# Pooled differences in PSUM, accumulating weight transfers from negated raw weights, and one scaling operation for two conv halves, in a one-core decoder layer

## The chip, the cores and the metric

The kernel runs on one core of one Trainium2 chip. The metric is the device time of one execution in microseconds, the median of the runs. A core has TensorE (PE, with PEld for its weight loads), VectorE (DVE), ScalarE (ACT), GpSimd (POOL) and SyncE (SP); each engine works through its own queue in order.

## The reference

One inference step of a one-layer trunk on 288 tokens: 256 of a new sequence, and 8 requests with 4 tokens each that carry a history. All in fp32.

```python
h = rmsnorm(x, norm1_g)
proj = h @ w_in + b_in                       # 2048 -> 1024 a, 1024 gate, 1024 z
u = a * sigmoid(gate)
c = silu(layernorm(depthwise_causal_conv([hist_conv, u], conv_w, conv_b), ln_g, ln_b))   # 31 taps
# z in 4 groups of 256 channels, windows 2, 4, 8, 16:
d = (sum of the last w of [hist_pool, z]) / min(w, position + 1) - z
p = (d @ pool_w[group]) * pool_scale
x = x + [c, p] @ w_out                       # 2048 -> 2048
f = relu(rmsnorm(x, norm2_g) @ w_ff1) ** 2   # 2048 -> 8192
x = x + f @ w_ff2
y = rmsnorm(x, norm_f)
```

The outputs are y and the last rows of [hist_conv, u] and [hist_pool, z].

## The kernel before, in words

Channels lie on the 128 partitions and the 288 tokens (T) along the free axis. Each fp32 product is made of three products of a narrower type, F32R: every weight tile and every activation is split into a high half `hi` (a cast) and a low half `lo` (the value less `hi`), and `gemm` (matmuls on line 292) adds hi x hi, lo x hi and hi x lo in PSUM. A matmul takes a 128x128 weight tile and 128x288 activations.

Weights come as raw halves of 128x1024, loaded by SyncE's queue (`load`), and are split by `split_part`. The cast to `hi` is always ScalarE's (line 260). The letter in the table WAYS says who makes `lo`: G is two GpSimd subtractions of 128x512 (line 269), V one VectorE subtraction (line 265), and D negates `hi` on ScalarE (line 262) and then lets a transfer issued by GpSimd read the raw half again from memory and add it (line 263). A product of the first layer takes four halves, so "GDGV" for c6 gives a way to each of its four. There are twelve D halves: one in c3 and c4, two in p3, c5, p2 and p1, one in c6 and p0. The raw and the split tiles come from pools of 6 and 5 buffers, so a weight is split as soon as TensorE has done with the one five before.

The first layer's products follow a written list:

```python
SEQUENCE = [(_s[0], int(_s[1])) for _s in "c0 c1 c2 c3 c4 p3 c5 p2 P3 c6 p1 P2 p0 P1 c7 P0".split()]
```

c_i is the product of conv pair i (128 channels of a in one bank, 128 of gate in the other), p_g that of pool group g, P_g the product of group g's pooled differences with `pool_w`. A c or p product has 96 matmuls, a P product 12. P1 runs inside c7, between its blocks (`between`), and P0 inside the first product of the output projection. All matmuls up to there are held in program order (`chain`); some products take their first matmuls in an order written by hand (TURN: c2, c5, the first of the projection, and others).

After c_i, `conv_pair` scales both banks by the row 1/rms (`rb`, line 434, two VectorE operations of 128x288), makes the sigmoid and u, and `taps` adds the 31 taps of the convolution, 30 VectorE operations of 128x256 (line 459), and those of the 32 sample tokens through a GpSimd product `prd` (line 463) and a VectorE reduction (line 465). The taps have a late priority and fill VectorE's gaps.

After p_g, `pool_group` scales (line 482), adds the bias into `z_all` (lines 485, 486), and GpSimd doubles the windows: sums `s` of 2, 4, 8, 16 (line 491). Then come a correction of the first positions, the scaling of the new samples' sums (line 497) and their difference into `d` (line 498). VectorE writes the other 256 tokens of `d` (line 500), ScalarE casts `d` to `dh` (line 502), VectorE subtracts to `dl` (line 503). `d` is an SBUF tile of the tag "ag2". `pool_products` multiplies and evacuates the two banks `pp` (lines 514 and 515, one ScalarE and one VectorE operation for each).

PSUM holds two tiles of two banks for products (`acc`), the tap sums and c1's banks (`cvp`), and a single tile of two banks with the tag "ms" for the pool products and the norms' sums.

A framework schedules the program: it keeps the data dependencies and lays out each engine's instructions by priority and by times that it models. The order on an engine is fixed when the kernel is built. `issue_after` pins one instruction behind another. After this stage (some 215 us) come the rest of the output projection and the feed-forward part in four chunks; the diff doesn't touch them.

Of the kernel before, what the change touches and what calls it, by code (L numbers as in the profile page):

```python
# [9 lines left out]
F32 = mybir.dt.float32  # L10
F32R = mybir.dt.float32r
AF = mybir.ActivationFunctionType
# [4 lines left out]
P = 128  # L17
D = 2048
# [51 lines left out]
TURN = "110100" * 4 + "01" * 6 + "1100" * 3  # L70


WAYS = {"c2": "GVGV", "c3": "GDGG", "c4": "GGGD", "c5": "GDGD", "c6": "GDGV", "c": "GGGV", "p0": "GDVG", "p": "GDDG", "w0": "GV", "w": "GG", "ff": "VV"}


VEC = (("norm1_g", 16), ("b_in", 24), ("conv_b", 8), ("ln_g", 8), ("ln_b", 8), ("pool_scale", 8), ("norm2_g", 16), ("norm_f", 16))
# [10 lines left out]
def trunk_kernel(ctx: ExitStack, tc: tile.TileContext, io):  # L87
# [18 lines left out]
    def nm(s):  # L106
        seen[s] = seen.get(s, 0) + 1
        return f"{s}{seen[s]}"
# [22 lines left out]
    def ms(name):  # L131
        return msp.tile([P, 2, 512], F32, name=nm(name), tag="ms")

    def f32(t):
        return t.bitcast(F32)

    def both(r):

        return r[:, None, :T].to_broadcast([P, 2, T])
# [114 lines left out]
    def split_part(raw, src, hi, lo, way):  # L254

        nc.scalar.copy(hi, raw)  # L260
        if way == "D":
            nc.scalar.activation(lo, f32(hi), AF.Copy, scale=-1.0)
            added.append(nc.gpsimd.dma_start(lo, src, accum_op=ALU.add))
        elif way == "V":
            nc.vector.tensor_tensor(lo, raw, f32(hi), op=ALU.subtract)  # L265
        else:
            for j in range(0, raw.shape[1], 2):
                with tc.issue_after(pooled[-1].ins) if pooled else nullcontext():
                    nc.gpsimd.tensor_tensor(lo[:, j : j + 2, :], raw[:, j : j + 2, :], f32(hi[:, j : j + 2, :]), op=ALU.subtract)  # L269
# [27 lines left out]
    def gemm(banks, rhs, m_outer=False, between={}, classes="", by_part=False, gets=None, pairs=None, late=0):  # L297


        n = len(rhs)  # L300
        gets = gets or ready.pop(0)
        todo, begins = [], {}
        if by_part:
            for k in range(0, n, 2):
                sets = [range(len(banks))] if k else [range(2), range(2, len(banks))]
                for last, ms_ in enumerate(sets, 1 - len(sets)):
                    for part, (w, x) in enumerate(((0, 0), (1, 0), (0, 1))):
                        if last == 0:
                            begins[len(todo)] = (k, None, k + 1)[part]
                        todo += [(k + (1 - d if x else d), m, w, x) for m in ms_ for d in range(2)]  # L310
        else:
            pairs = pairs or [(k, m) for k in range(0, n, 2) for m in range(len(banks))]
            if m_outer:
                pairs.sort(key=lambda km: km[1])
            for k, m in pairs:
                begins[len(todo)] = (k, m) if m else k
                todo += [(k + d, m, w, x) for d, w, x in ((0, 0, 0), (1, 0, 0), (0, 1, 0), (1, 1, 0), (1, 0, 1), (0, 0, 1))]
        todo[:late] = sorted(todo[:late], key=lambda p: p[2])
        head = todo[: len(classes)]
        for j, c in enumerate(classes):  # L320
            todo[j] = next(p for p in head if c == "." or (p[0] + p[3]) % 2 == int(c))
            head.remove(todo[j])
        ends = {m: [f(j for j, p in enumerate(todo) if p[1] == m) for f in (min, max)] for m in range(len(banks))}
        ahead = None
        for j, (k, m, w, x) in enumerate(todo):
            if begins.get(j) in between:
                ahead = between[begins[j]]()
            with tc.issue_after(ahead.ins) if ahead is not None and not chain else nullcontext():
                last = mm(banks[m][:, :T], gets[k // 8](k % 8, m)[w], rhs[k][x], start=j == ends[m][0], stop=j == ends[m][1])
        ready.extend(itertools.islice(weights, 1))  # L330
        return last.ins

    def bank2():
        return acc.tile([P, 2, 512], F32, name=nm("ac"), tag="ac")

    def each(bk):
        return [bk[:, m, :] for m in range(2)]
# [84 lines left out]

    def conv_products(i, **kw):
        history(i)
        banks = each(bank2())
        gemm(banks, hx, **kw)
        return banks

    def conv_pair(i, banks):
        up = u_all[:, i, 0:UO]  # L430
        us = samples(u_all[:, i, UO:UL], US)
        ta, gate = [b[:, :T] for b in banks]
        for b in (gate, ta):
            nc.vector.tensor_tensor(b, b, rb, op=ALU.mult)
        tg = tmpp.tile([P, 2, T], F32, name=nm("tg"), tag="ag", bufs=2)[:, 0, :]
        nc.scalar.activation(tg, gate, AF.Sigmoid, bias=v("b_in", 8 + i))
        for out, a, b in ((up[:, CH:UO], ta[:, :SEQ], tg[:, :SEQ]), (us[:, :, CH:US], samples(ta[:, SEQ:T], NS), samples(tg[:, SEQ:T], NS))):
            nc.vector.scalar_tensor_tensor(out=out, in0=a, scalar=v("b_in", i), in1=b, op0=ALU.add, op1=ALU.mult)
        if i % 2 == 0:
            cs.append(actp.tile([P, 2, T], F32, name=nm("c"), tag="c", bufs=4))  # L440
        while waiting:
            taps(*waiting.pop())
        if i in (2, 3):
            waiting.append((i, up, us))
        else:
            taps(i, up, us)
# [24 lines left out]
                    nc.gpsimd.tensor_tensor(sum_c[:, 0, :], sum_c[:, 0, :], part, op=ALU.add)  # L471


    dd = {}

    def pool_group(g):
        nc.sync.dma_start(z_all[:, 2 * g : 2 * g + 2, ZO:ZL], io["hist_p"][:, 2 * g : 2 * g + 2, :])
        bk = bank2()
        gemm(each(bk), hx)
        z = z_all[:, 2 * g : 2 * g + 2, :]  # L480
        tz = tmpp.tile([P, 2, T], F32, name=nm("tz"), tag="ag", bufs=2)
        nc.vector.tensor_tensor(tz, bk[:, :, :T], both(rb), op=ALU.mult)
        for m in range(2):
            b_in = v("b_in", 16 + 2 * g + m)
            nc.scalar.activation(z[:, m, PH:ZO], tz[:, m, 0:SEQ], AF.Identity, bias=b_in)
            nc.scalar.activation(samples(z[:, m, ZO:ZL], ZS)[:, :, PH:ZS], samples(tz[:, m, SEQ:T], NS), AF.Identity, bias=b_in)
        s, w = z, 1
        while w < WINDOWS[g]:
            s2 = tmpp.tile([P, 2, ZL], F32, name=nm("s"), tag="s", bufs=2)
            for m in range(2):  # L490
                nc.gpsimd.tensor_tensor(s2[:, m, 2 * w - 1 :], s[:, m, 2 * w - 1 :], s[:, m, w - 1 : ZL - w], op=ALU.add)  # L491
            s, w = s2, 2 * w
        d = tmpp.tile([P, 2, T], F32, name=nm("d"), tag="ag2", bufs=2)
        first_sums = s[:, :, PH : PH + w - 1]
        nc.gpsimd.tensor_tensor(first_sums, first_sums, rcnt[:, None, w - 2 : 2 * w - 3].to_broadcast([P, 2, w - 1]), op=ALU.mult)
        news = [x[:, :, ZO:ZL].rearrange("p m (b t) -> p m b t", t=ZS)[:, :, :, PH:] for x in (s, z)]
        nc.gpsimd.tensor_scalar(news[0], news[0], 1.0 / w, None, op0=ALU.mult)
        last = nc.gpsimd.tensor_tensor(d[:, :, SEQ:T].rearrange("p m (b t) -> p m b t", t=NS), news[0], news[1], op=ALU.subtract)
        newest[g] = last
        nc.vector.scalar_tensor_tensor(out=d[:, :, 0:SEQ], in0=s[:, :, PH:ZO], scalar=1.0 / w, in1=z[:, :, PH:ZO], op0=ALU.mult, op1=ALU.subtract)  # L500
        dh, dl = act2("dx", tag="p", bufs=4)
        nc.scalar.copy(dh, d)
        nc.vector.tensor_tensor(dl, d, f32(dh), op=ALU.subtract)  # L503
        dd[g] = dh, dl
# [12 lines left out]

    for i in range(2):
        history(i)
    pair0 = each(bank2())  # L520
    pair1 = [cvp.tile([P, 512], F32, name=nm("ac"), tag="cv") for m in range(2)]

    def first_row():
# [2 lines left out]
    chain.append(gemm(pair0 + pair1, hx, between={15: first_row}, classes="01" * 18 + TURN, by_part=True))  # L526
    third = conv_products(2, classes=TURN)
    nc.gpsimd.memset(z_all[:, :, 0:PH], 0.0)
    conv_pair(0, pair0)
    conv_pair(1, pair1)  # L530
    conv_pair(2, third)
    def ahead(n):

        while len(ready) < n + 1:
            ready.extend(itertools.islice(weights, 1))
        return ready.pop(n)

    for kind, i in SEQUENCE[3:-1]:
        if (kind, i) == ("P", 1):
            continue  # L540
        if i == 7:
            pooled.append(newest[1])
        if kind == "c":
            conv_pair(i, conv_products(i, classes=TURN if i == 5 else "", **(dict(gets=ahead(1), between={8: lambda: pool_products(1)}) if i == 7 else {})))
        elif kind == "p":
            pool_group(i)
        else:
            pooled.append(newest[i])
            pool_products(i)
    pooled.append(newest[0])  # L550
    proj = [halves(dd[k // 2])[k % 2] for k in korder]
    bks = [bank2() for _ in range(2)]
# [248 lines left out]
```

## Time and profile before

| | before |
|---|---|
| median of 3 runs | 1084.95 us (1084.92 to 1085.11) |
| profiled execution | 1083.8 us, its span 1082.0 us |
| granted TensorE clock | 0.998 |
| busy: PE, DVE, ACT, POOL | 1068.6, 632.2, 484.2, 179.8 us |
| GpSimd's transfers (queue q0) | 1728 packets, 6.29 MB |

The span is from the first to the last instruction of the profiled execution. Its own time is 1.15 us under the median of the runs, so sums made on the profile are set against 1083.8 and then carried to the median as differences. Times in rows are microseconds from the start of the span. A window's row gives its length, TensorE's busy time with the count of matmuls, the granted clock, the share of time that the transfer engines were busy, and GB/s.

### The profile page before, as it was taken

What the parts mean: (1) busy time and instruction counts of PE and PEld (TensorE: products, weight loads), DVE (VectorE), ACT (ScalarE), POOL (GpSimd) and SP (SyncE); (2) the same over time, 40 slices, a digit from 0 to 9 for tenths busy, and PEclk for the clock granted to TensorE, in tenths of its full rate; (3) what the DMA queues carried; (4) which work ended last, traced back from release to release, by engine and by line L of the source; (5) the groups of instructions that cost most, each with busy time, mean ns of one, the idle gap of its engine ahead of it and who ended that gap; (6) DMA issues with size and microseconds to landing.
All of it is one profiled execution on the core that took longest, in us unless ns stands there. A gap on an engine that the chain in (4) does not pass through costs nothing.

```text
span 1082.0 us, 19548 instructions
## 1 busy us (share of the span) xinstructions
PE 1068.6 (99%) x8176; PEld 1067.0 (99%) x8176; DVE 632.2 (58%) x804; ACT 484.2 (45%) x593; POOL 179.8 (17%) x189
## 2 busy tenths in 40 slices
PE   9999999999999999999999999999999999999996
PEld 8999999999999999999999999999999999999996
DVE  8899998788655544444544444545544445554552
ACT  8655555565544433334443333444433334444441
POOL 1898889612000000000000000000000000000001
PEclk9999999999999999999999999999999999999999
DMA  9898778555555555555555555555555555555522
GB/s 328 279 267 222 198 173 249 189 168 170 170 169 165 174 171 163 174 168 165 175 171 163 173 168 166 173 172 164 172 171 163 173 172 163 172 169 166 172 79 88
DMA packets 59017, 193.34 MB, mean 179 GB/s; under 512 B 6320, under 2 KB 11312, under 8 KB 58928
## 3 DMA queue, kind: packets, MB, share of 16 engines
q1 hardware_dynamic: 56336, 184.35, 54.4%
q0 software_dynamic: 1728, 6.29, 3.2%
q8 instruction: 64, 1.05, 0.4%
q10 hardware_dynamic: 864, 1.44, 0.4%
q14 instruction: 25, 0.20, 0.1%
HBM read 187.78 MB, written 4.28 MB: 177 GB/s over the span
## 4 chain that ended last, share of the span: by engine, by line
PE 75%; issue 20%; DVE 2%; DMA 1%; POOL 1%; ACT 0%; SPq 0%; POOLq 0%; DVEq 0%
PE ac L292 74%; DMA wlo<-in_w 1%; DMA wr<-in_w 1%; DVE pc L459 1%; PE pp L292 0%; POOL wlo L269 0%; DVE wlo L265 0%; POOL s L491 0%; POOL xT L737 0%; DVE dx L503 0%; DVE z_all L409 0%; SPq L191 0%; ACT z_all L407 0%; DVE wlo L360 0%; DVE c L465 0%
## 5 line engine op out<-in xcount | busy, mean ns | idle before, releaser
L260 ACT CAST whi<-wr 128x1024 fp32r<-128x1024 f32 (+1 forms) x332 | 346.7, 1044 | 549.9 <-PE ac L292 538.3
L265 DVE TENSOR_TENSOR wlo<-wr,whi 128x1024 fp32r<-128x1024 f32 x282 | 348.3, 1235 | 348.0 <-ACT whi L260 348.0
L292 PE MATMUL ac<-ax,whi 128*128 128x288 f32 x2048 | 351.0, 292 | 0.0
L292 PE MATMUL ac<-fx,whi 128*128 128x288 f32 x2048 | 350.2, 292 | 0.0
L292 PEld LDWEIGHTS ac<-ax,whi 128*128 128x128 f32 x2048 | 296.1, 187 | 0.0
L292 PEld LDWEIGHTS ac<-fx,whi 128*128 128x128 f32 x2048 | 295.5, 187 | 0.0
L292 PE MATMUL ac<-ax,wlo 128*128 128x288 f32 x1024 | 217.4, 292 | 0.0
L292 PE MATMUL ac<-fx,wlo 128*128 128x288 f32 x1024 | 216.4, 292 | 0.0
L292 PEld LDWEIGHTS ac<-ax,wlo 128*128 128x128 f32 x1024 | 162.6, 187 | 0.0
L292 PEld LDWEIGHTS ac<-fx,wlo 128*128 128x128 f32 x1024 | 162.2, 187 | 0.0
L737 POOL TENSOR_TENSOR xT<-xT,rf 128x288 f32<-128x288 f32 x4 | 3.1, 793 | 799.9 <-ACT rf L741 799.9
L292 PE MATMUL ac<-hx,whi 128*128 128x288 f32 x768 | 131.1, 294 | 1.3 <-DVE hx L354 1.3
L292 PEld LDWEIGHTS ac<-hx,whi 128*128 128x128 f32 x768 | 111.6, 188 | 1.7 <-ACT hx L356 1.5
L269 POOL TENSOR_TENSOR wlo<-wr,whi 128x512 fp32r<-128x512 f32 x76 | 103.7, 1449 | 21.8 <-ACT whi L260 20.3
L459 DVE SCALAR_TENSOR_TENSOR pc<-u_all,vec,pc 128x256 f32<-128x256 f32 x232 | 100.1, 482 | 3.5 <-ACT pc L456 1.9
L292 PE MATMUL ac<-hx,wlo 128*128 128x288 f32 x384 | 80.4, 295 | 2.0 <-DMA wlo<-in_w 1.7
L292 PEld LDWEIGHTS ac<-hx,wlo 128*128 128x128 f32 x384 | 60.7, 188 | 2.7 <-DMA wlo<-in_w 2.2
L292 PE MATMUL ac<-dx,whi 128*128 128x288 f32 x256 | 46.2, 295 | 0.0
L292 PE MATMUL ac<-mx,whi 128*128 128x288 f32 x256 | 44.5, 292 | 0.0
L679 DVE SCALAR_TENSOR_TENSOR t<-ac,r 128x576 f32<-128x576 f32 x32 | 24.2, 758 | 25.4 <-PE ac L292 25.3
L292 PEld LDWEIGHTS ac<-dx,whi 128*128 128x128 f32 x256 | 38.2, 188 | 0.2
L292 PEld LDWEIGHTS ac<-mx,whi 128*128 128x128 f32 x256 | 37.4, 187 | 0.0
(129 smaller groups left out, 541.7 us busy)
## 6 DMA issues: line engine op xcount, KB each, us to landing
wr<-in_w SPq DMA_DIRECT2D x335, 512.0 KB, 3.8
wlo<-in_w POOLq DMA_DIRECT2D x12, 512.0 KB, 7.7
xT<-in_xT SPq DMA_DIRECT2D x8, 288.0 KB, 7.2
wr<-in_w SPq DMA_DIRECT2D x5, 256.0 KB, 4.8
out_u_out<-u_all SPq DMA_DIRECT2D x1, 1208.0 KB, 10.1
u_all<-in_hist_c SPq DMA_DIRECT2D x8, 136.0 KB, 5.8
out_z_out<-z_all SPq DMA_DIRECT2D x1, 668.0 KB, 8.7
z_all<-in_hist_p SPq DMA_DIRECT2D x4, 152.0 KB, 8.4
```

What stands on the lines that cost most here:

```text
L260: nc.scalar.copy(hi, raw)
L265: nc.vector.tensor_tensor(lo, raw, f32(hi), op=ALU.subtract)
L269: nc.gpsimd.tensor_tensor(lo[:, j : j + 2, :], raw[:, j : j + 2, :], f32(hi[:, j : j + 2, :]), op=ALU.subtract)
L292: last = nc.tensor.matmul(*args, **kw)
L459: nc.vector.scalar_tensor_tensor(out=dst, in0=up[:, w : w + SEQ], scalar=cwv[:, w : w + 1], in1=pc, op0=ALU.mult, op1=ALU.add)
L679: nc.vector.scalar_tensor_tensor(out=t, in0=bk[:, :, :T], scalar=0.0, in1=both(rows2[0]), op0=ALU.max, op1=ALU.mult)
L737: eng.tensor_tensor(xk, xk, r[:, None, :].to_broadcast([P, n, T]), op=ALU.mult)
```

## The change

- `split_part`, way D: `lo` is the negated raw half, written ahead of the cast to `hi`; before, it was the negated `hi`, written behind it. The transfer that adds the raw half onto `lo` stays.
- WAYS: the entry of c6 is gone, so that c6 takes "GGGV" of "c": its second half goes from D to G.
- `conv_products` and `conv_pair`: where both banks lie in one tile, one VectorE operation of 128x576 scales them. c1, whose banks are two tiles, stays as it was.
- `pool_group` ends with GpSimd's difference of the new samples, written into `s` itself. The rest goes to a new function `pool_means`: `d` is a PSUM tile of the tag "ms", ScalarE copies the new samples into it, VectorE writes the other tokens, and `dh` and `dl` are made from there.
- The means of group 3 follow p3; those of groups 2 and 1 follow the products P3 and P2; those of group 0 follow P1. P1 runs ahead of block 4 of c7; before, it ran ahead of block 8.

```diff
-WAYS = {..., "c5": "GDGD", "c6": "GDGV", "c": "GGGV", ...}
+WAYS = {..., "c5": "GDGD", "c": "GGGV", ...}
...
+        if way == "D":
+            nc.scalar.activation(lo, raw, AF.Copy, scale=-1.0)
         nc.scalar.copy(hi, raw)
         if way == "D":
-            nc.scalar.activation(lo, f32(hi), AF.Copy, scale=-1.0)
             added.append(nc.gpsimd.dma_start(lo, src, accum_op=ALU.add))
...
-        ta, gate = [b[:, :T] for b in banks]
-        for b in (gate, ta):
-            nc.vector.tensor_tensor(b, b, rb, op=ALU.mult)
+        if isinstance(banks, list):
+            ta, gate = [b[:, :T] for b in banks]
+            for b in (gate, ta):
+                nc.vector.tensor_tensor(b, b, rb, op=ALU.mult)
+        else:
+            nc.vector.tensor_tensor(banks[:, :, :T], banks[:, :, :T], both(rb), op=ALU.mult)
+            ta, gate = [banks[:, m, :T] for m in range(2)]
...
-        last = nc.gpsimd.tensor_tensor(d[:, :, SEQ:T]..., news[0], news[1], op=ALU.subtract)
-        newest[g] = last
-        nc.vector.scalar_tensor_tensor(out=d[:, :, 0:SEQ], in0=s[:, :, PH:ZO], scalar=1.0 / w, in1=z[:, :, PH:ZO], op0=ALU.mult, op1=ALU.subtract)
+        newest[g] = nc.gpsimd.tensor_tensor(news[0], news[0], news[1], op=ALU.subtract)
+        sums[g] = s, z, news[0], 1.0 / w
+
+    def pool_means(g):
+
+        s, z, fresh, scale = sums[g]
+        d = ms("d")[:, :, :T]
+        nc.scalar.copy(d[:, :, SEQ:T].rearrange("p m (b t) -> p m b t", t=NS), fresh)
+        nc.vector.scalar_tensor_tensor(out=d[:, :, 0:SEQ], in0=s[:, :, PH:ZO], scalar=scale, in1=z[:, :, PH:ZO], op0=ALU.mult, op1=ALU.subtract)
         dh, dl = act2("dx", tag="p", bufs=4)
         nc.scalar.copy(dh, d)
         nc.vector.tensor_tensor(dl, d, f32(dh), op=ALU.subtract)
...
+    def last_pool():
+
+        pool_products(1)
+        pool_means(0)
...
-            conv_pair(i, conv_products(i, ..., **(dict(gets=ahead(1), between={8: lambda: pool_products(1)}) if i == 7 else {})))
+            conv_pair(i, conv_products(i, ..., **(dict(gets=ahead(1), between={4: last_pool}) if i == 7 else {})))
         elif kind == "p":
             pool_group(i)
+            if i == 3:
+                pool_means(3)
         else:
             pooled.append(newest[i])
             pool_products(i)
+            pool_means(i - 1)
```

More of the change, by code (lines that the diff above doesn't have):

```diff
@@ L70 @@
 TURN = "110100" * 4 + "01" * 6 + "1100" * 3
-WAYS = {"c2": "GVGV", "c3": "GDGG", "c4": "GGGD", "c5": "GDGD", "c6": "GDGV", "c": "GGGV", "p0": "GDVG", "p": "GDDG", "w0": "GV", "w": "GG", "ff": "VV"}
+WAYS = {"c2": "GVGV", "c3": "GDGG", "c4": "GGGD", "c5": "GDGD", "c": "GGGV", "p0": "GDVG", "p": "GDDG", "w0": "GV", "w": "GG", "ff": "VV"}
 VEC = (("norm1_g", 16), ("b_in", 24), ("conv_b", 8), ("ln_g", 8), ("ln_b", 8), ("pool_scale", 8), ("norm2_g", 16), ("norm_f", 16))
@@ L424, in conv_products @@
         history(i)
-        banks = each(bank2())
-        gemm(banks, hx, **kw)
-        return banks
+        bk = bank2()
+        gemm(each(bk), hx, **kw)
+        return bk
     def conv_pair(i, banks):
@@ L471, in taps @@
                     nc.gpsimd.tensor_tensor(sum_c[:, 0, :], sum_c[:, 0, :], part, op=ALU.add)
-    dd = {}
+    dd, sums = {}, {}
     def pool_group(g):
@@ L492, in pool_group @@
             s, w = s2, 2 * w
-        d = tmpp.tile([P, 2, T], F32, name=nm("d"), tag="ag2", bufs=2)
         first_sums = s[:, :, PH : PH + w - 1]
@@ L497, in pool_group @@
         nc.gpsimd.tensor_scalar(news[0], news[0], 1.0 / w, None, op0=ALU.mult)
-        last = nc.gpsimd.tensor_tensor(d[:, :, SEQ:T].rearrange("p m (b t) -> p m b t", t=NS), news[0], news[1], op=ALU.subtract)
-        newest[g] = last
-        nc.vector.scalar_tensor_tensor(out=d[:, :, 0:SEQ], in0=s[:, :, PH:ZO], scalar=1.0 / w, in1=z[:, :, PH:ZO], op0=ALU.mult, op1=ALU.subtract)
+        newest[g] = nc.gpsimd.tensor_tensor(news[0], news[0], news[1], op=ALU.subtract)
[5 more added lines that the diff above has]
+        nc.vector.scalar_tensor_tensor(out=d[:, :, 0:SEQ], in0=s[:, :, PH:ZO], scalar=scale, in1=z[:, :, PH:ZO], op0=ALU.mult, op1=ALU.subtract)
         dh, dl = act2("dx", tag="p", bufs=4)
@@ L519, in trunk_kernel @@
         history(i)
-    pair0 = each(bank2())
+    first_bank = bank2()
+    pair0 = each(first_bank)
     pair1 = [cvp.tile([P, 512], F32, name=nm("ac"), tag="cv") for m in range(2)]
@@ L528, in trunk_kernel @@
     nc.gpsimd.memset(z_all[:, :, 0:PH], 0.0)
-    conv_pair(0, pair0)
+    conv_pair(0, first_bank)
     conv_pair(1, pair1)
@@ L543, in trunk_kernel @@
         if kind == "c":
-            conv_pair(i, conv_products(i, classes=TURN if i == 5 else "", **(dict(gets=ahead(1), between={8: lambda: pool_products(1)}) if i == 7 else {})))
+            conv_pair(i, conv_products(i, classes=TURN if i == 5 else "", **(dict(gets=ahead(1), between={4: last_pool}) if i == 7 else {})))
         elif kind == "p":
             pool_group(i)
+            if i == 3:
+                pool_means(3)
         else:
```

## The prediction

> **What bounds the kernel now.** I read the page's busy shares first, then TensorE's waits, then a table of windows over the first 200 us.
>
> ```profile
> span 1082.0 us, 19548 instructions
> PE 1068.6 (99%) x8176; PEld 1067.0 (99%) x8176; DVE 632.2 (58%) x804; ACT 484.2 (45%) x593; POOL 179.8 (17%) x189
> ```
>
> TensorE is busy 99% of the span, and the change takes no matmul away. Only two things can move the time: matmuls that wait, and matmuls that run at a slower pace. The waits of the weight loads on TensorE:
>
> ```profile
> PEld ac L292 <- DMA wlo<-in_w: 2.2, 2, 1.6
> PEld ac L292 <- ACT hx L356: 1.5, 1, 1.5
> ```
>
> The second row lies in the start, which the diff doesn't touch. The first is two waits, 2.2 us together, 1.6 and so 0.6 us, on a transfer into `wlo`: the transfers that add raw weights onto a negated half (way "D", line 263). The windows show the pace:
>
> ```profile
> core 0: us, PE busy (x), PEclk, DMA share, GB/s
> 32.30:77.10 44.80, 44.80 (x346) 1.00 0.88 260
> 86.50:113.20 26.70, 26.70 (x208) 1.00 0.84 216
> 114.90:127.60 12.70, 12.70 (x95) 1.00 0.83 217
> 128.30:173.50 45.20, 45.20 (x339) 1.00 0.75 209
> 175.00:199.40 24.40, 24.40 (x190) 1.00 0.75 205
> 400.00:600.00 200.00, 200.00 (x1541) 1.00 0.55 169
> ```
>
> Dividing time by count: 0.1295 us a matmul before 77, 0.1284 before the first wait, then 0.1337 and 0.1333 in the two windows after the waits, then 0.1284 again and 0.1298 in the long steady part. The granted clock is 1.00 in all of them, so it isn't the clock. Against 0.1298 the two slow windows lose 95 x 0.0039 = 0.37 and 339 x 0.0035 = 1.19 us, about 1.5 together. They begin at the waits and end where the product before 175 runs in the hand-written order TURN. I read the slow pace as something that a wait brings and TURN ends. So what depends on these two waits is 2.2 + 1.5 = 3.7 us; nothing else in the span that the diff touches costs TensorE time.
>
> **The change part by part.** *c6's transfer becomes a GpSimd subtraction.* The queues of GpSimd, ScalarE and VectorE around the waits, in order of time (start, duration, engine, line, operation, idle time before it and what ended it):
>
> ```profile
> 101.94 3.10 POOL L269 TENSOR_TENSOR wlo<-wr,whi 128x512 fp32r<-128x512 f32 x2 [0.93 <-ACT whi L260]
> 105.00 2.20 POOL L463 TENSOR_TENSOR prd<-u_all,vec 128x992 f32<-128x992 f32 x1
> 107.15 0.88 POOL L263 DMA_DIRECT2D wlo<-in_w  x1
> 107.81 2.80 POOL L269 TENSOR_TENSOR wlo<-wr,whi 128x512 fp32r<-128x512 f32 x2
> 112.67 3.51 POOL L269 TENSOR_TENSOR wlo<-wr,whi 128x512 fp32r<-128x512 f32 x2 [2.06 <-ACT whi L260]
> 116.14 1.74 POOL L491 TENSOR_TENSOR s<-z_all 128x422 f32<-128x422 f32 x2
> 119.51 0.88 POOL L263 DMA_DIRECT2D wlo<-in_w  x1
> ```
>
> ```profile
> 102.35 1.05 ACT L260 CAST whi<-wr 128x1024 fp32r<-128x1024 f32 x1 [0.48 <-PE ac L292]
> 104.55 1.05 ACT L262 ACTIVATE wlo<-whi 128x1024 fp32r<-128x1024 f32 x1
> 115.49 0.50 ACT L514 ACTIVATE dx<-pp,vec 128x288 fp32r<-128x288 f32 x1 [1.66 <-DVE dx L515]
> 115.89 1.04 ACT L260 CAST whi<-wr 128x1024 fp32r<-128x1024 f32 x1
> 116.97 1.06 ACT L262 ACTIVATE wlo<-whi 128x1024 fp32r<-128x1024 f32 x1
> 105.77 2.05 DVE L503 TENSOR_TENSOR dx<-d,dx 128x576 fp32r<-128x576 f32 x1
> 113.06 1.97 DVE L265 TENSOR_TENSOR wlo<-wr,whi 128x1024 fp32r<-128x1024 f32 x1
> ```
>
> Then a piece of the chain of waits (start, duration), the first of the two waits, and the landing times over all twelve transfers:
>
> ```profile
> 119.51 8.72 DMA wlo<-in_w
> ...
> 114.85 0.30 PEld L292 LDWEIGHTS ac<-hx,wlo 128*128 128x128 f32 x2 [1.59 <-DMA wlo<-in_w]
> ...
> DMA to landing us min/median/max: 6.3/7.7/10.1
> ```
>
> The ninth transfer is c6's: negated at 104.55, issued at 107.15 behind `prd`, waited for until 114.85. The change drops it: the half is cast at 102.35 and GpSimd subtracts in two operations (2.80 us by the 107.81 row) after 105.0, or after 107.2 if `prd` goes first: done by 110.0, 3 us ahead of its use (114.85 - 1.6 = 113.25). The first wait goes: -1.6, and -0.37 of pace behind it. Price: GpSimd gains 2.8 - 0.9 = 1.9 us, ScalarE loses 1.06. GpSimd sat idle 2.06 us before 112.67, which takes it; without that cover p1's first half and p1's transfers behind it come 1.9 later.
>
> *Negation from raw, ahead of the cast.* The instruction count is the same; `lo` is ready one cast (1.05) earlier and `hi` 1.06 later. Eleven halves. `hi` has room: in c6 it was cast at 102.35 and used after 113. For p1's first transfer TensorE now wants the data at 128.27 - 0.6 - 1.6 - 0.37 = 125.7. If ScalarE keeps its place, `lo` ends at 115.89 + 1.06 = 116.95; issued at once or behind the two sums (1.74), with 8.72 to landing, it lands at 125.7 to 127.4. But ScalarE stood there 1.66 us for the VectorE queue (the 115.49 row), and that queue gets shorter, next.
>
> *d in PSUM.* Removed: nothing in count but GpSimd's write target. Added: four ScalarE copies of 128x64, by the 128x32 row below 0.31 each, 1.3 us in all on an engine at 45%. VectorE's subtraction L503 now takes one operand from PSUM:
>
> ```profile
> L503 DVE TENSOR_TENSOR dx<-d,dx 128x576 fp32r<-128x576 f32 x4 | 5.7, 1427 | 0.0
> L482 DVE TENSOR_TENSOR tz<-ac,rb 128x576 f32<-128x576 f32 x4 | 3.0, 748 | 0.4 <-PE ac L292 0.4
> L434 DVE TENSOR_TENSOR ac<-ac,rb 128x288 f32<-128x288 f32 x16 | 7.1, 457 | 1.3 <-PE ac L292 1.3
> L486 ACT ACTIVATE z_all<-tz,vec 128x32 f32<-128x32 f32 x8 | 2.5, 313 | 0.0
> 149.37 0.74 DVE L503 TENSOR_TENSOR dx<-d,dx 128x576 fp32r<-128x576 f32 x1
> ```
>
> The nearest row with a PSUM operand and this size is L482, 0.75. Bounds: no gain (1.43 stays) and 1.43 - 0.75 = 0.68 each, 2.7 in all; I take 0.75, as the row is the same shape. The one that matters is at 105.77: 2.05 becomes 0.75, so the queue behind it moves up 1.3 us, to L515 and with it the ScalarE cast at 115.89.
>
> The Trainium skill, SBUF — State Buffer, Who interferes with whom, says that a VectorE operation with two SBUF inputs contends with GpSimd reading SBUF, and one with at most one SBUF input doesn't. The trace agrees in part: the 2.05 us row ends as `prd` on GpSimd does, yet the 149.37 row took 0.74 beside GpSimd subtractions. By the rule the four would cost 0.75 each; by the mean row they stay at 1.43.
>
> *Conv halves in one operation.* Seven pairs: 2 x 0.457 become one like L482, 0.748: 0.17 saved each, 1.2 in all on VectorE, off the path. The operation now waits for both banks; VectorE has taps (line 459) to run meanwhile.
>
> *Means after products; P1 at block 4 of c7 rather than 8.* d now shares the one PSUM tile of the tag "ms" with the pool products, so a group's means start when the former group's products are evacuated. P2's last evacuation, group 1's means, P1's first product and last evacuation, P0's first product:
>
> ```profile
> 142.83 0.51 DVE L515 SCALAR_TENSOR_TENSOR dx<-pp,vec,dx 128x288 fp32r<-128x288 f32 x1
> 146.13 0.33 POOL L498 TENSOR_TENSOR d<-s,z_all 128x64 f32<-128x64 f32 x1
> 146.78 1.49 DVE L500 SCALAR_TENSOR_TENSOR d<-s,z_all 128x512 f32<-128x512 f32 x1
> 148.36 0.67 ACT L502 CAST dx<-d 128x576 fp32r<-128x576 f32 x1 [1.10 <-DVE d L500]
> 158.49 0.43 PE L292 MATMUL pp<-dx,whi 128*128 128x288 f32 x2
> 169.69 0.43 PE L292 MATMUL pp<-dx,whi 128*128 128x288 f32 x2
> 164.93 0.50 DVE L515 SCALAR_TENSOR_TENSOR dx<-pp,vec,dx 128x288 fp32r<-128x288 f32 x1
> ```
>
> P2's evacuation ends at 143.34, before group 1's sums end (146.46), so the tile is free in time. The chain from there to the end of the 149.37 row took 3.65; with the copy 4.0, so 150.5 if nothing moves up. P1 moves up by 24 matmuls (3.1) and by the gain: 158.49 - 3.1 - 3.7 = 151.7. That leaves 1.2 us, more where the sums, which follow TensorE, move up too. P0's means now wait for P1's evacuation: that took 165.43 - 158.49 = 6.9, so 151.7 + 6.9 + 4.0 = 162.6, against P0's products at 169.69 - 3.7 = 166.0. So both cost nothing; if that cover were gone each microsecond late is one on TensorE. The sums' tiles `s` are held longer, but the next writer of the same buffer comes two tiles later. Behind the four copies on ScalarE stand weight casts; they have some 10 us of room.
>
> **Sum.** 1.6 + 0.6 + 1.5 = 3.7 us if both waits go. The profiled execution took 1083.8 (its span 1082.0), 1.15 below the median 1084.95; the same gain off the median gives 1081.3.
>
> **The rivals.**
> 1. *p1's transfer stays late.* For it: GpSimd carries 1.9 us more just ahead, and the landing is 125.7 to 127.4 against 125.7 if ScalarE doesn't move. Against it: the 1.3 us on VectorE. A wait of 0 to 1.7 remains, middle 0.5, and the slow pace of 1.19 behind it stays. Gain 1.6 + 0.37 + 0.6 - 0.5 = 2.1, with 0.9 to 2.6 as ends: 1082.9 (1082.4 to 1084.1).
> 2. *No difference.* The engine orders are planned anew, and another transfer gets late (they take from 6.3 to 10.1 us, and the spread is larger than either wait): the wait of 1.6 and its pace only change place. 1084.9, between 1084.1 and 1085.8.
> 3. *Slower: P1's products wait for means.* Place: block 4 of c7. The single PSUM tile puts evacuation, copy, mean, cast and subtraction in series on two in-order queues. It decides once `dl` of group 1 ends later than 151.7 + 3.7 + 2.2 = 157.6, 7 us behind the 150.5 above: a chain as slow as P1's evacuation (6.9) instead of 4.0 isn't enough alone, it also needs the evacuation of P2 4 us later. At 9 us late TensorE loses 9 - 1.2 = 7.8, less the 3.7: 1089.
> 4. *The pace doesn't follow the waits.* Both waits go, the 1.5 stays: 1082.7. The windows speak against it, as the fast pace ends at both waits.
>
> **How the numbers follow.** This kernel's runs tell about 0.2%, 2.2 us, from no change: the bounds are 1082.8 and 1087.1. Forecast 0.40, at 1081.3; if the pace comes down to 0.1284 the 1.5 is 95 x 0.0053 + 339 x 0.0049 = 2.2, which gives 1080.6, and if only half of the 1.5 comes it is 1082.0. Rival 1 0.28; rival 4 0.06; rival 2 0.14; rival 3 and anything like it 0.12. The range from 1080.6 to 1085.0 takes in the first three and half of rival 2: 0.81. Faster: 0.40, 0.11 of rival 1 and 0.05 of rival 4, 0.56. Slower 0.12, same 0.32.
>
> **What would show it.** Right: no row of TensorE waiting for `wlo` from a transfer; some 0.130 a matmul from 86 to 173; eleven transfers, c6's half from line 269; L503's 128x576 near 0.75; P1's products near 152. Wrong: a `wlo` wait near 126 with 0.133 behind it (rival 1), a `wlo` wait elsewhere (2), a wait of TensorE on `dx` (3), or 0.133 with no wait ahead of it (4).

## The result, and the profile after

The changed kernel took 1081.27 us in the median (1079.98 to 1083.85), the kernel before 1084.93 measured beside it: a ratio of 0.9971 (95% interval 0.9961 to 0.9980), 3.7 us less. The profiled execution took 1079.98 us against 1083.8, 3.8 less; its span fell from 1082.0 to 1078.2. Executions at a granted clock of 0.752, which take some 1319 us whatever the kernel, are left out of the ratios (the medians count them and would move by 0.1 us at most), and two profiles that were taken in such executions, the first of experiment 1 and that of experiment 7, aren't read.

```profile
span 1078.2 us, 19544 instructions
PE 1066.2 (99%) x8176; PEld 1065.0 (99%) x8176; DVE 627.4 (58%) x797; ACT 482.5 (45%) x596; POOL 178.6 (17%) x190
```

The waits of the weight loads (total, times, longest, all in us):

```profile
PEld ac L293 <- ACT hx L357: 1.8, 1, 1.8
PEld warm L214 <- DVE cst L231: 1.0, 1, 1.0
PEld ac L293 <- DVE wlo L361: 0.5, 1, 0.5
PEld ends L748 <- DVE cst L745: 0.2, 1, 0.2
```

No row names a transfer into `wlo`; what is left lies in the start and the end. The pace, in windows that can be held against those of before (length, TensorE's busy time and matmuls, clock, transfer share, GB/s):

```profile
114.90:127.60 12.70, 12.70 (x100) 1.00 0.95 243
128.30:165.00 36.70, 36.70 (x285) 1.00 0.75 200
175.00:190.00 15.00, 15.00 (x117) 1.00 0.60 195
400.00:600.00 200.00, 200.00 (x1540) 1.00 0.52 169
```

12.70 us now hold 100 matmuls where they held 95, and from 128 to 165 a matmul takes 36.7 / 285 = 0.1288 us where it took 0.1333 (from start to start, 130.0 ns and 133.3). The stage runs at the speed of the steady part.

Counting the matmuls through places the gain. The 800th starts at 109.60 us where it started at 109.82, and the 1320th at 177.30 where it started at 181.14; from there to the end the distance stays. So 3.6 of the 3.8 us were gained between these two, where both waits and the slow pace had been.

GpSimd around p1's two transfers, and ScalarE ahead of them (start, duration, operation, idle before):

```profile
102.76 2.67 POOL L468 TENSOR_TENSOR prd<-u_all,vec 128x992 f32<-128x992 f32 x1
105.39 5.04 POOL L270 TENSOR_TENSOR wlo<-wr,whi 128x512 fp32r<-128x512 f32 x4
111.51 2.55 POOL L270 TENSOR_TENSOR wlo<-wr,whi 128x512 fp32r<-128x512 f32 x2 [1.08 <-ACT whi L262]
114.86 0.80 POOL L473 TENSOR_TENSOR sum_c<-c,c 128x288 f32<-128x288 f32 x1
116.46 0.87 POOL L264 DMA_DIRECT2D wlo<-in_w  x1
117.95 1.14 POOL L264 DMA_DIRECT2D wlo<-in_w  x1
```

```profile
112.79 1.06 ACT L261 ACTIVATE wlo<-wr 128x1024 fp32r<-128x1024 f32 x1
113.76 0.48 ACT L524 ACTIVATE dx<-pp,vec 128x288 fp32r<-128x288 f32 x1
114.14 1.04 ACT L262 CAST whi<-wr 128x1024 fp32r<-128x1024 f32 x1
```

c6's half is made by GpSimd between 105.39 and 107.9. p1's first negation ends at 113.85 where it ended at 118.03, 4.2 us earlier: 1.07 from standing ahead of the cast, the rest because the cast itself moved from 115.89 to 114.14, no longer behind a wait for VectorE, and the negation sits ahead of P3's second evacuation. The transfer is issued at 116.46, 3.0 us earlier than the 119.51 of before. By the landing events it lands at 124.74, 0.72 us ahead of its first use; p1's second has 0.64 us, p2's second 0.39 and p3's second, the closest, 0.12. So the stage has no wait, but little to spare.

VectorE's and ScalarE's rows for the new `d`, and the transfers' landing times:

```profile
L438 DVE TENSOR_TENSOR ac<-ac,rb 128x576 f32<-128x576 f32 x7 | 5.3, 764 | 2.5 <-PE ac L293 2.5
L513 DVE TENSOR_TENSOR dx<-d,dx 128x576 fp32r<-128x576 f32 x4 | 3.0, 749 | 0.0
L512 ACT CAST dx<-d 128x576 fp32r<-128x576 f32 x4 | 2.5, 634 | 1.6 <-DVE d L510 1.6
L509 ACT COPY d<-s 128x64 f32<-128x64 f32 x4 | 0.8, 209 | 0.0
```

```profile
DMA to landing us min/median/max: 5.5/9.2/11.2
```

### The profile page after: what moved, and what is told of

The parts are those of the page before. It is cut to its first block, busy times and chain, and to the rows that moved or that the text cites. A ratio compares the mean times of both kernels' runs of the same rounds, so it can differ in the third digit from the quotient of the medians.

```text
span 1078.2 us, 19544 instructions
## 1 busy us (share of the span) xinstructions
PE 1066.2 (99%) x8176; PEld 1065.0 (99%) x8176; DVE 627.4 (58%) x797; ACT 482.5 (45%) x596; POOL 178.6 (17%) x190
## 3 DMA queue, kind: packets, MB, share of 16 engines
q8 instruction: 64, 1.05, 0.4%
## 4 chain that ended last, share of the span: by engine, by line
PE 77%; issue 20%; DMA 1%; ACT 0%; DVE 0%; POOL 0%; SPq 0%; POOLq 0%; DVEq 0%
PE ac L293 77%; DMA wr<-in_w 1%; PE pp L293 1%; POOL xT L756 0%; ACT hx L357 0%; ACT whi L352 0%; DVE z_all L410 0%; ACT z_all L408 0%; DVE wlo L361 0%; PE norm L293 0%; SPq L191 0%; POOLq L806 0%; DVE xT L729 0%; ACT whi L359 0%; PE pmean L293 0%
```

## The experiments

The ratio behind each time is to the kernel before, timed beside it.

Where two profiles are compared, one thing has to be taken off. The kernel's start and p3's transfers, which lie ahead of the two waits, take up to 2 us more in one execution than in another, and all rows behind them then stand that much later. An execution's lateness below is how much later its 800th matmul starts than that of the profile of before (109.82); the changed kernel's is -0.2 us.

**1. c6's half alone** (1087.16 us, ratio 1.0023, 1.0014 to 1.0033):

```diff
-WAYS = {..., "c6": "GDGV", "c": "GGGV", ...}   # before
+WAYS = {..., "c": "GGGV", ...}
```

> The kernel before, with c6's second half going from D to G and nothing else. Theory: the two waits stand one behind the other. The first (1.6 us, c6) goes, and TensorE then comes 2.0 us earlier to p1's transfer, whose place on ScalarE and GpSimd hasn't moved, so that wait grows from 0.6 to about 2.5 us: the time falls by 0 to 0.5 us (1084.4 to 1084.9), and the slow pace behind p1 stays. Rival: each wait costs by itself; the first is simply gone: 2.0 us faster (1082.9), p1's wait still 0.6.

Both expected times fall: the edit alone makes the kernel 2.4 us slower. A second run gives its trace:

> The kernel before with c6's half going from D to G, for one look at its trace: its runs were 2.4 us slower than before. Theory: the 1.9 us that GpSimd gains comes just ahead of p1's two transfers, which are issued that much later, while TensorE comes 2.0 us earlier: p1's wait is 4 to 5 us where it was 0.6, and no wait at c6. Rival: the time is lost elsewhere (a wait on dx, on pp, or at p0), p1's wait 2.5 us or less.

It took 1088.34 us. The waits, the two long ones, and GpSimd's issues:

```profile
PEld ac L292 <- DMA wlo<-in_w: 6.7, 4, 2.8
```

```profile
130.04 0.30 PEld L292 LDWEIGHTS ac<-hx,wlo 128*128 128x128 f32 x2 [2.56 <-DMA wlo<-in_w]
147.22 0.30 PEld L292 LDWEIGHTS ac<-hx,wlo 128*128 128x128 f32 x2 [2.75 <-DMA wlo<-in_w]
```

```profile
120.46 0.89 POOL L263 DMA_DIRECT2D wlo<-in_w  x1
131.57 0.81 POOL L468 TENSOR_TENSOR sum_c<-sum_c,c 128x288 f32<-128x288 f32 x1 [2.39 <-DVE c L459]
138.26 0.86 POOL L263 DMA_DIRECT2D wlo<-in_w  x1
```

c6's wait is gone and the others grew: p1's from 0.6 to 2.56, and p0's, which wasn't there, is 2.75. p3's two, 0.85 and 0.57, lie ahead of c6; with the start they make this execution 1.7 us late at the 800th matmul. At the 950th, behind p1's wait, it is 1.8 late: what c6's wait gave back, p1's took, as the first theory had it. GpSimd's extra work at c6 was covered: p1's negation on ScalarE starts 1.8 us later than before (118.75 against 116.97), which is the lateness, and its transfer is issued 0.95 later (120.46 against 119.51). What makes the edit slower is p0. Its transfer is issued 3.1 us later (138.26 against 135.12), 1.4 more than the lateness, and it takes 8.9 us to land where it took 6.3. The order on GpSimd changed: the sum of the conv outputs (L468), which stood behind `prd` just ahead of that transfer (134.37), now stands ahead of `prd` and waits 2.39 us for VectorE. My theory placed 4 to 5 us at p1 and missed p0; the rival's 2.5 at p1 and a wait at p0 is what happened. Removing one wait of a chain passed it on, and the new order added another.

**2. The new negation alone** (1083.02 us, 0.9983, 0.9975 to 0.9992):

```diff
+        if way == "D":
+            nc.scalar.activation(lo, raw, AF.Copy, scale=-1.0)
         nc.scalar.copy(hi, raw)
         if way == "D":
-            nc.scalar.activation(lo, f32(hi), AF.Copy, scale=-1.0)
```

> The kernel before, with the negation made from the raw half ahead of the cast and nothing else. In this program's GpSimd queue c6's transfer still stands behind prd, and p1's first transfer stands one sum operation earlier. Theory: c6's wait keeps its 1.6 us (it was GpSimd's queue, not ScalarE, that held the issue back), p1's 0.6 us goes as the landing is 1 to 1.6 us earlier, the slow pace behind c6's wait stays: 0.4 to 0.8 us faster (1084.1 to 1084.5). Rival: every D half lands 1.05 us earlier, so that both waits shrink: 1.6 us or more faster (1083.3 or less).

```profile
103.99 2.21 POOL L464 TENSOR_TENSOR prd<-u_all,vec 128x992 f32<-128x992 f32 x1
106.14 0.88 POOL L264 DMA_DIRECT2D wlo<-in_w  x1
...
142.09 0.30 PEld L293 LDWEIGHTS ac<-hx,wlo 128*128 128x128 f32 x2 [1.80 <-DMA wlo<-in_w]
```

The rival was right: c6's and p1's waits are both gone, though c6's transfer still stands behind `prd`; the queue ahead of it runs 1.0 us earlier, as GpSimd's subtractions ahead of `prd` no longer wait 0.93 us for a cast on ScalarE. From the 800th to the 980th matmul (some 136 us) this execution gains 2.7 us, as much as the changed kernel does there. Then one wait of 1.80, at p0, takes 1.6 of it back, and the slow pace holds behind it. p0's transfer was issued 2.35 us earlier than before (132.77 against 135.12), but took 9.3 us to land where it took 6.3; why isn't shown. So the negation edit is worth 1.8 us alone.

**3. Both weight edits, without pools and conv halves** (1082.01 us, 0.9978, 0.9969 to 0.9988): experiments 1 and 2 together.

> The kernel before with both edits of the weight split (c6's half to G, negation from the raw half ahead of the cast), without the edits to the pools and the conv halves. Theory: c6's wait goes, p1's transfer is issued some 1 us earlier but TensorE comes 2.0 us earlier, and VectorE's queue isn't shortened, so that p1's wait stays at 0 to 1 us with the slow pace behind it: 1.5 to 2.6 us faster than before (1082.2 to 1083.3), not the 3.7 of the whole change. Rival: the weight edits are all of the gain: 3.5 us or more (1081.3).

Between the two: 2.8 us, some three quarters of the change, though its interval overlaps that of the changed kernel. Its trace has no wait on a transfer at all, and 194 matmuls in the window from 140 to 165 us, against 189 before. From the 800th to the 1200th matmul (some 165 us) it gains 3.5 us, as much as the changed kernel does there. What it has, and the changed kernel hasn't, are two waits in the output projection, at 170 and 179 us, which with the slow pace behind them lose 1.7 us in this execution:

```profile
PEld ac L293 <- issue: 0.6, 1, 0.6
PEld ac L293 <- DVE xT L599: 0.6, 1, 0.6
```

With c6's half alone 2.4 us slower and the negation alone 1.8 faster, the two together are 2.8 faster: the effects don't add, as each moves the same chain. What the edits to the pools and conv halves do against these two waits wasn't tried apart.

**4. The changed kernel with the old negation** (1086.67 us, 1.0018, 1.0008 to 1.0027): experiment 2's edit taken back.

> The changed kernel with the negation back behind the cast, from the cast half. Theory: p1's first transfer landed 0.72 us ahead of its use in the changed kernel; 1.06 us later on ScalarE and behind one more sum on GpSimd it is 0.3 to 1.5 us late, and the slow pace (up to 1.2 us) follows: 1 to 2.7 us slower than the changed kernel, 1082.3 to 1084.0. Rival: with VectorE's queue shorter the order on ScalarE doesn't matter: 1081.3.

It is 5.4 us slower than the changed kernel and slower than before; the expected direction, twice the upper end. The waits:

```profile
PEld ac L292 <- DMA wlo<-in_w: 3.1, 3, 2.5
```

```profile
118.12 1.06 ACT L262 ACTIVATE wlo<-whi 128x1024 fp32r<-128x1024 f32 x1
120.60 0.87 POOL L263 DMA_DIRECT2D wlo<-in_w  x1
```

p1's negation ends 5.3 us later than in the changed kernel and not 1.06. This execution is 1.7 us late at the 800th matmul, and so 1.9 behind the changed kernel; for the other 3.4 the planner put the negation, and the casts around it, behind P3's evacuation on ScalarE again. Behind the wait of 2.54 us comes the slow pace (189 matmuls in 25 us), and in this execution one thing more, which a window from 130 to 134 us shows:

```profile
130.00:134.00 4.00, 4.00 (x19) 0.57 0.87 263
134.00:140.00 6.00, 6.00 (x47) 1.00 0.52 170
```

The granted clock fell to half for 3.4 us: some 15 matmuls took 240 ns from start to start, 1.6 us lost. From the 800th matmul on this execution is 5.1 us longer than the changed kernel: 2.5 of wait, 1.6 of clock, 1.0 of slow pace. Whether the clock fell in the other executions isn't shown.

**5. All but the weight edits** (1084.08 us, 0.9993, 0.9984 to 1.0001): the changed kernel with experiments 1's and 2's edits taken back.

> The changed kernel without its two edits of the weight split (c6 keeps its D half, the negation comes from the cast half, behind it): d in PSUM, the means after the products, P1 at block 4 and the conv halves in one operation are in. Theory: c6's wait of 1.6 us stays, as prd still stands ahead of its transfer; VectorE's queue is some 1.3 us shorter ahead of p1's transfer, so that p1's wait of 0.6 us shrinks or goes; slow pace stays: 0 to 0.7 us faster (1084.2 to 1084.9). Rival: the means and the earlier P1 are worth time by themselves: 1.5 us or more faster.

The time is within what was expected, and not told apart from no change, but the way there was another: c6's wait is gone without either weight edit. Two waits are left, one of them new:

```profile
PEld pp L292 <- DVE dx L512: 0.6, 1, 0.6
PEld ac L292 <- DMA wlo<-in_w: 0.5, 1, 0.5
103.33 2.21 POOL L467 TENSOR_TENSOR prd<-u_all,vec 128x992 f32<-128x992 f32 x1
105.49 0.87 POOL L263 DMA_DIRECT2D wlo<-in_w  x1
```

The first is P3's products waiting for `dl`, the kind of wait that my slower rival put at P1. The second is p1's transfer. c6's transfer still stands behind `prd`, but `prd` starts at 103.33 where it started at 105.00, and the transfer lands 2.6 us ahead of its use.

**6. d back in SBUF** (1083.01 us, 0.9983, 0.9974 to 0.9991):

```diff
-        d = ms("d")[:, :, :T]
+        d = tmpp.tile([P, 2, T], F32, name=nm("d"), tag="ag2", bufs=2)
```

> The changed kernel with d back in an SBUF tile; the order of GpSimd's queue is the same as in the changed kernel, and the means still follow the products. Theory of the prediction: the subtraction of 128x576 takes up to 2.05 us beside prd again, VectorE's queue is 1.3 us longer ahead of p1's transfer, which had 0.72 us of room: a wait of about 0.6 and up to 1.2 of slow pace, 1082.0 to 1083.1. Rival: the place of d costs nothing that TensorE sees: 1081.3 within 0.3.

```profile
L513 DVE TENSOR_TENSOR dx<-d,dx 128x576 fp32r<-128x576 f32 x4 | 4.3, 1087 | 0.0
```

```profile
118.03 0.88 POOL L264 DMA_DIRECT2D wlo<-in_w  x1
...
126.59 0.30 PEld L293 LDWEIGHTS ac<-hx,wlo 128*128 128x128 f32 x2 [0.35 <-DMA wlo<-in_w]
...
140.00:165.00 25.00, 25.00 (x190) 1.00 0.70 174
```

As the theory had it, the subtraction takes 1.09 on the mean instead of 0.75 (1.58 in the first, beside `prd`), p1's transfer is issued 1.57 us later, a wait of 0.35 appears and the slow pace behind it. The way from the one to the other isn't the theory's. 0.7 of the 1.57 is lateness: ScalarE's negation for p1 starts that much later too (113.50 against 112.79). The rest is GpSimd's:

```profile
111.99 1.22 DVE L266 TENSOR_TENSOR wlo<-wr,whi 128x1024 fp32r<-128x1024 f32 x1
112.22 3.40 POOL L270 TENSOR_TENSOR wlo<-wr,whi 128x512 fp32r<-128x512 f32 x2 [0.56 <-ACT whi L262]
```

VectorE's weight subtraction stands 1.94 us later than in the changed kernel (111.99 against 110.05), 1.2 more than the lateness, and now runs beside GpSimd's pair, which takes 3.40 us where it took 2.55. That the one lengthens the other is read from these rows and not tried apart. Nor does `d` in SBUF make p1's transfer late by itself: in experiments 2 and 3, with the means where they were, it lies in SBUF too, and the transfer lands 0.81 and 0.45 us ahead of its use. The medians differ by 1.7 us; the two intervals overlap slightly (0.9974 to 0.9991 against 0.9961 to 0.9980), so the profile carries this more than the time. The Trainium skill, SBUF — State Buffer, Who interferes with whom, has a VectorE operation with two SBUF inputs contend with GpSimd's reads and one with a single SBUF input not; the pair of L513 rows, 1.09 against 0.75 with GpSimd's queue in the same order, agrees. But it doesn't happen each time: of the four in SBUF one, at 149.17, took 0.74 beside GpSimd subtractions.

**7. c6's half back to D in the changed kernel** (1080.76 us, 0.9961, 0.9947 to 0.9975):

```diff
-WAYS = {..., "c": "GGGV", ...}   # changed kernel
+WAYS = {..., "c6": "GDGV", "c": "GGGV", ...}
```

> The changed kernel with c6's second half back to D; the queues of the engines differ from the changed kernel's in a handful of rows. Theory of the prediction: c6's transfer stands behind prd and lands at 112.5 to 114.5 against a use at 113.0: a wait of 0 to 1.5 with up to 1.2 of slow pace: 0.5 to 2.5 us slower than the changed kernel. Second theory (from the run with the new negation alone, where c6's transfer landed 0.46 ahead of its use): the new negation alone was enough for c6, and the D half spares GpSimd 1.9 us: within 0.5 us of the changed kernel.

The second theory holds: with the new negation c6 needs no G. This edit is worth nothing that was measured.

**8. P1 back at block 8** (1080.73 us, 0.9962, 0.9950 to 0.9975):

```diff
-between={4: last_pool}
+between={8: last_pool}
```

> The changed kernel with P1 and group 0's means back ahead of block 8 of c7. GpSimd's queue is the same. Theory: no wait of TensorE on means or evacuations was there before or after, so nothing changes: within 0.5 us of the changed kernel (1081.3). Rival: the earlier P1 frees the single PSUM tile in time for group 0; at block 8 P0's products wait for dx: 1 us or more slower.

No wait on means, 195 matmuls from 140 to 165 us, and 3.6 us gained between the 800th and the 1320th matmul, as in the changed kernel: P1's place costs and brings nothing.

**9. Two scalings for a conv pair** (1081.28 us, 0.9969, 0.9957 to 0.9981):

```diff
-        if isinstance(banks, list):
+        if True:
-            ta, gate = [b[:, :T] for b in banks]
+            ta, gate = [b[:, :T] for b in (banks if isinstance(banks, list) else each(banks))]
```

> The changed kernel with two scaling operations of 128x288 for each conv pair. The cost itself is 7 x 0.17 = 1.2 us on VectorE, off TensorE's path. Theory: it shows only if the longer VectorE queue takes the 0.7 us of room that p1's and p0's transfers have: 0 to 1.5 us slower than the changed kernel (1081.3 to 1082.8). Rival: one operation for two is worth nothing by itself, 1081.3 within 0.3; a change over 2 us would mean that the order planned anew has moved a transfer, and not the 1.2 us.

The same as the changed kernel, to 0.01 us in the medians, with 3.6 us gained in the stage again. 1.2 us of VectorE in seven places don't reach TensorE.

**10. The pace: TURN on p0 in the kernel before** (1084.29 us, 0.9993, 0.9984 to 1.0002):

```diff
-        gemm(each(bk), hx)
+        gemm(each(bk), hx, classes=TURN if g == 0 else "")
```

> The kernel before, with the first matmuls of p0 in the order TURN and nothing else; both waits stay. Theory: the slow pace that follows a wait ends at a product with TURN, so the window from 140 to 170 us runs at 0.130 instead of 0.1333 us a matmul, and the time falls by some 230 x 0.0035 = 0.8 us (1084.1). Rival: TURN has nothing to do with it (the slow pace belongs to what the other engines do in that stage): 0.1333 stays and the time is that of before, within 0.2 us.

The time moved by 0.5 us, which its interval doesn't tell from nothing. The profile tells more: the windows from 140 to 165 us of the kernel before and of this one:

```profile
140.00:165.00 25.00, 25.00 (x189) 1.00 0.68 163
```

```profile
140.00:165.00 25.00, 25.00 (x194) 1.00 0.71 160
```

This execution waited on transfers four times, 2.7 us in all (0.28 and 0.38 at p3, 1.3 at c6, the last until 129.6 at p1), and yet ran p0's rest and c7 at 0.1289 us a matmul and not 0.1323. TURN ends the slow pace.

**11. TURN on p0 and c7 in the changed kernel** (1081.17 us, 0.9963, 0.9950 to 0.9975): experiment 10's edit, and `i in (5, 7)` for `i == 5` in c's product.

> The changed kernel with TURN on the first matmuls of p0 and c7; the queues of the other engines are the same as in the changed kernel. Theory: in the executions in which a p1 or p0 transfer is late by chance, the slow pace (133.3 against 130.0 ns from start to start) ends at the next of these two products and not at the projection: 0.2 to 0.8 us faster than the changed kernel in the median (1080.5 to 1081.1), and 130 ns from 155 us on in any profile. Rival: at a pace that is already fast TURN costs or spoils it: the same or slower.

No difference in the median. 194 matmuls stand in the window where 195 stand without TURN, and from the 800th to the 1320th matmul it gains 3.4 us where experiments 8 and 9 gain 3.6: at a fast pace TURN does little harm, 0.2 us in this profile, and there was no wait for it to repair. None of 7, 8 and 11, the lowest medians, is told apart from the changed kernel, so no version was found that beats it.

The pace over all profiles, from 140 to 165 us: with a wait of 0.35 us or more between 112 and 130 us and no TURN behind it, 189, 189, 189 and 190 matmuls (before, experiments 4, 5 and 6); where a wait fell inside the window, 177 in 23.43 us and 169 in 22.48 (0.132 and 0.133; experiments 2 and 1); with no wait, 194 or 195 (the changed kernel, experiments 3, 8, 9 and 11); with waits and TURN, 194 (experiment 10). From start to start a matmul takes 130.0 ns in the one state and 133.3 in the other.

## Why the prediction was right

- *What the gain hangs on.* Two waits of 2.2 us and 1.5 us of slow pace behind them, 3.7 in all: the median moved by 3.7 and the profile by 3.8, 3.6 of it between the two places named, with no wait on a transfer left and the fast pace throughout. That a wait brings the slow pace and TURN ends it, read from six windows, holds between 110 and 175 us in all twelve profiles, most plainly in experiments 6 and 10. The windows' counts take in some two matmuls that overlap the ends, so that a short window reads too fast: 0.1284 and 0.1298 are the same pace, 130 ns from start to start, and the case of 1080.6 had no ground. And the pace wasn't fast ahead of the second wait, as rival 4 says; the first wait had ended it.
- *Some luck in the size.* The forecast read one profile of the kernel before. In three of the five profiles with the old negation (experiments 1, 4 and 10) p3's two transfers are late too, by 0.5 to 1.4 us together; in none of the seven with the new one. So the edit is worth more in some executions than the two waits show, and that the median agrees to a tenth of a microsecond is in part chance.
- *c6's half.* The term -1.6 -0.37 was put on the wrong edit. G removes c6's wait, but alone it costs 2.4 us (experiment 1), and in the changed kernel it can be taken back (experiment 7). Its price on GpSimd was covered as forecast; what it cost came at p0, by a changed order on GpSimd that the forecast didn't look for.
- *The negation.* I priced it at one cast, 1.05 us, and doubted whether that was enough for p1. It is the edit that counts most: 1.8 us alone, 5.4 us when taken out (5.1 by the one profile, 1.6 of it the clock). The step that was mis-sized is "if ScalarE keeps its place": it doesn't, the order on ScalarE is planned anew, and p1's negation ended 4.2 us earlier, not 1.06.
- *d in PSUM.* 0.75 for the subtraction was forecast and 0.749 measured; the copies were 0.21 each, not 0.31. (The 2.05 us row that I read as ending with `prd` ends 0.6 us behind it.) The 1.3 us on VectorE did reach p1's transfer, but in experiment 6 not by L515 and ScalarE's cast, as the argument against rival 1 had it: by the rows, a VectorE subtraction came to stand beside GpSimd's.
- *Conv halves and P1's place.* Both priced at nothing on the path, and both are (experiments 8 and 9). P1's products came at 151.85, forecast 151.7.
- *Rivals.* Rival 1, p1's transfer staying late, is what happens in the changed kernel without the edit of d; rival 4, the pace not following, is excluded; rival 3's wait on means appeared for 0.6 us, at P3, in experiment 5 only. Rival 2, another transfer late in a new order, is what happens to p0 in experiments 1 and 2.

So the sum was right and its split over the edits was not. p1's transfer was made ready late on ScalarE. c6's was ready there at 105.60 and stood behind `prd` on GpSimd until 107.15, as the forecast read it; but that queue was late itself, and each of three edits brought it forward or emptied it: G, the new negation (experiment 2) and the pools (experiment 5).

## What to carry to other kernels

Where TensorE is 99% busy and waits twice, look at when each late transfer became ready and not at the wait that shows: taking the first wait away alone moved it on to the next transfer, and the order that came with the edit cost time at a third. Price a step in a planned queue by the places it may take, not by its own length, since an edit of one operation moved another by 4 us. Before a row of one profile is set against that of another, take off how late the whole execution runs there. And count a stall with what follows it: here a wait of 0.35 us was enough for about 1 us of slower matmuls behind it.

## What the hardware did that was not expected

The pace has two values, 130.0 and 133.3 ns from start to start, at a granted clock of 1.00 in both; in the slow one every fourth matmul starts some 10 ns late. After a wait on weights in the middle of the stage the slow value held until the next TURN; after the wait in the kernel's start it came in some executions and not in others (133.3 between 18 and 31 us before, 130.2 in the changed kernel, with waits of 1.5 and 1.8 us there). What in the chip makes the two paces wasn't found.

A wait can also cost the clock. In experiment 4 the 2.54 us were followed by 3.4 us at half clock, while two waits of 2.56 and 2.75 us in experiment 1 weren't. The Trainium skill, TensorE: Matmul & The Clock Gate, Part 1: The HAM clock gate, says that the array falls to half rate after an idle window of about 3.4 us, and that the window runs freely. The length of the slow stretch agrees. The gap doesn't: 2.5 us is shorter than the page's figure, and can't leave a window of 3.4 us idle throughout wherever it lies. Why it was enough here and a longer one in experiment 1 wasn't is open.

The time that the transfers took to land varied by more than the waits: 9.2 us in the median in the changed kernel and 7.7 before, so that part of the earlier issue was lost again. p2's second landed at 101.67 where it had landed at 99.95, though it was issued 1.3 us earlier. It isn't the earlier issue or the new negation alone: with the old one the profiles of experiments 1 and 4 have 9.2 and 9.1, that of experiment 10 has 8.4. What sets it wasn't tried.
